# Neighbouring residual tiles summed for the feed forwards, and their first up columns taken by quarters

## The chip, the cores and the metric

The kernel runs on one core of one Trainium2 chip. The metric is the device time of one execution in microseconds (us), the median of several. All arithmetic is fp32. The engines are TensorE (PE in the profile: matmul, and PEld: the load of its weights), VectorE (DVE), ScalarE (ACT), GpSimd (POOL) and SyncE (SP, which here only issues transfers). SBUF is the on-chip memory that the engines work in, PSUM the banks that matmuls write to.

## The reference

A decoder trunk for 512 tokens of width 1024, with two layers. Layer 0 mixes with a gated DeltaNet, layer 1 with sliding-window attention; both attend to 256 memory tokens. Each layer ends with a SwiGLU feed forward:

```python
def swiglu(h, w_gate_up, w_down):
    gu = h @ w_gate_up
    return (jax.nn.silu(gu[..., :D_FF]) * gu[..., D_FF:]) @ w_down
...
        x = x + jnp.concatenate([mix_out.astype(x.dtype), mem_o.astype(x.dtype)], axis=-1) @ w_out[layer]
        x = x + swiglu(rms_norm(x, ln_ffn[layer]), w_gate_up[layer], w_down[layer])
```

D_FF is 2816, so there are 22 gate columns and 22 up columns of 128. The change touches the output projection (w_out), whose rows complete the residual x, and the feed forward behind it.

## The kernel before, in words

The residual is held transposed as eight tiles x0 to x7 of 128 features by 512 tokens. Each value that TensorE multiplies is split in a high part (whi, h, T from ScalarE) and a low part (wlo, l, a second T: the value less its high part, on VectorE), and each product is three matmuls: high by high, low of the data by high, high by low of the weights. A plain column is 8 steps over the features, so 24 matmuls of 128x512 into one bank.

Most of the feed forward goes "by quarters" (`sevens`): two columns, two halves of the features and two halves of the tokens are combined so that seven products of 128x256 do the work of eight. It needs sums of the data and of the weights. The data's sums are made by `token_sums(j)`, once per layer for four pairs of residual tiles: x_j with x_{j+4}. One call scales half of a tile (Tbh), makes four combined quarters by scalar_tensor_tensor (Tah, Tal: the two raw tiles of one pair, not parts of a split), and splits them in high parts (ScalarE) and low parts (VectorE), both named T. The weights' sums are made partly by transfers that add what they bring to a tile in SBUF (ws, issued from GpSimd's queue), partly by VectorE (wraw). The weight parts live in a ring of a few places, so that a new part can only be made when TensorE is through with an old one.

The first pair of columns is different. Its sums are not ready when the feed forward begins, so gate 0, up 0, gate 1 and up 1 are plain columns. After two steps of up 0 the squares of x, summed up (sqa) and split (ws), meet a tile of ones on TensorE, which gives the norm's rstd. Gate 0's result times rstd goes through silu (fg), the product with up is fu.

`output` computes the eight rows of w_out. In layer 1 five rows are begun before (n = 5). After each row come the residual's addition, the split of the scaled x (h, l), and the square with its addition (sq, sqa) on VectorE.

The program is recorded by a layer that sets its own order on each engine, from the dependencies and its costs; `nosync` adds a dependency of order alone. Each engine works through its own queue in order. So the order of instructions on each engine is fixed when the program is built, and only the times are found on the chip. `behind` holds weight loads on SyncE's queue back until a named instruction.

Of the kernel before, what the change touches and what calls it, by code (L numbers as in the profile page):

```python
# [9 lines left out]
F32 = mybir.dt.float32  # L10
# [8 lines left out]
P = 128  # L19
T = 512  # L20
# [64 lines left out]
class Builder:  # L85
# [980 lines left out]
    def output(self, xp, layer, mix, begun=()):  # L1066

        nc, a = self.nc, self.a
        self.weng = nc.vector
        h = []  # L1070
        self.acc = None
        hpool = self.apool if layer else self.bpool
        bank = lambda m: self.bank(("pj", "pj", "pt")[m % 3] if begun else "g" if m % 4 == 3 else "pj")
        n, ws, lows = len(begun), [], []

        def early(m):
            if begun and n <= m < KD:
                ws.append(self.weight(a["wout"][layer, m]))
                lows.append(self.low)

        done = [list(row)[-1] for row in begun]
        for i in range(2):
            early(n + i)
        for m in range(KD):
            ps = done[m] if m < n else list(
                self.row(layer, m, mix, lambda: bank(m), ws.pop(0) if ws else None))[-1]
            self.ended = self.tt(nc.vector, self.x[m], ps, self.x[m], ALU.add)
            if m >= n - 1:
                early(m + 3)
            hl = self.pair(hpool)  # L1090
            self.split_gain(self.x[m], self.gain(G_FFN[layer], m), *hl)
            if m == 0 and lows:
                self.nosync(self.low, lows[-1])
            h.append(hl)
            self.acc = self.accumulate(xp, self.acc, self.x[m], m)
        self.behind = self.loaded if layer else None
        return h

    def ffn8(self, fp, xp, layer, h, apool, rope=False):
# [121 lines left out]
            src = [a["wdn"][layer, m + i][:, f0 * P:(f0 + size) * P] for i in range(2)]  # L1221
            begin(self.sevens(fp, src, sums, ring, first, second, third, fourth, m == 0), none)

        def gate(f):
            ps = self.project(col(f, 0), h, "pj")
            if f == 0:
                list(zip(range(2), ups[0]))
                self.rstd_from(acc, *(self.t(fp, [P, T], F32R, "ws", 4) for _ in range(2)), after=self.last,
                               root=(self.cosT, self.sinT) if layer else None)
                self.use(SILU_SIN)  # L1230
            g = self.t(fp, [P, T], F32, "fg", 4)
            self.tt(nc.vector, g, ps, self.rstd, ALU.mult)
            self.fn(g, g, AF.Silu)
            return g

        f0 = 0
        for size in (8, 8, 6):
            acts, sums = [], []
            last = f0 + size == FT
            places.clear()  # L1240
            f = f0
            if f == 0:
                us, ups = [], [self.projected(col(i, 1), h, "g") for i in range(2)]
                made = act_sums()
                for i in range(2):
                    g = gate(i)
                    us.append(self.t(fp, [P, T], F32, "fu", 3))
                    if i:
                        hsums.append(self.token_sums(fp, layer, 2, h, True))
                    self.tt(nc.vector, us[i], list(ups[i])[-1], g, ALU.mult)  # L1250
                    for j in ((0, 1), (3,))[i]:
                        hsums.append(self.token_sums(fp, layer, j, h, True))
                for work in made:
                    work(*us)
                f = 2
            while f < f0 + size:
                g = columns(f, 0, (self.rstd, self.rstd), ("fg", 4), none, none, silu)
                columns(f, 1, g, ("fu", 3), *((none, none, whole) if last else act_sums(f + 2 == f0 + size)))
                f += 2
            if not last:  # L1260
                for m in range(0, KD, 2):
                    rows(m)
                    if rope and f0 + m == 0:
                        self.spread_tables()
                if f0 == 0:
                    self.t(fp, [P, 40], F32, "rest")
                f0 += size
# [57 lines left out]
    def token_sums(self, fp, layer, j, h, tags=None):  # L1325


        nc, q = self.nc, T // 2
        if j == 0:
            self.minus = self.t(fp, [P, 4], F32, "minus")  # L1330
            self.ts(self.minus, self.gains[:, G_FFN[layer] + 4:G_FFN[layer] + 8], -1.0, ALU.mult)
        g0, g1 = (self.gain(G_FFN[layer], j + i) for i in (0, 4))
        n1 = self.minus[:, j:j + 1]
        x0, x1 = self.x[j], self.x[j + 4]
        c = self.t(fp, [P, q], F32, *(("Tbh", 4) if tags else ("fc",)))
        raws = [self.t(fp, [P, T], F32, *((f"Ta{n}", 4) if tags else (f"ac{8 + j % 3}{n}",))) for n in "hl"]
        t = [raws[i // 2][:, i % 2 * q:(i % 2 + 1) * q] for i in range(4)]
        ins = nc.vector.tensor_scalar(out=c, in0=x0[:, q:], scalar1=g0, scalar2=None, op0=ALU.mult).ins
        if layer and j:

            self.nosync(ins, self.ended)
        self.stt(t[0], x0[:, :q], g0, c, ALU.mult, ALU.subtract)
        self.stt(t[1], x1[:, q:], n1, t[0], ALU.mult, ALU.subtract)
        self.stt(t[2], x1[:, q:], g1, c, ALU.mult, ALU.subtract)
        self.stt(t[3], x1[:, :q], n1, t[1], ALU.mult, ALU.subtract)
        hl = [self.t(fp, [P, D], F32R, "T", 8) for _ in range(2)]
        for i, raw in enumerate(raws):
            self.split(raw, *(x[:, i * T:(i + 1) * T] for x in hl))
        parts = {f"t{i + 1}": [x[:, i * q:(i + 1) * q] for x in hl] for i in range(4)}
        parts["11"] = [x[:, :q] for x in h[j]]  # L1350
        parts["21"], parts["22"] = ([x[:, i * q:(i + 1) * q] for x in h[j + 4]] for i in range(2))
        return parts

    def quarters(self, fp, src, sums, by, u, ring, *works):
# [24 lines left out]

        return self.sevens(fp, src, sums, ring, first, second, third, fourth)  # L1380

    def sevens(self, fp, src, sums, ring, first, second, third, fourth, late=False):

        nc = self.nc
        q, w = T // 2, len(sums) * P
        (a11, a12), (a21, a22) = ([c[:, :w], c[:, w:]] for c in src)
        a1 = self.load(src[0])
# [6 lines left out]
        nc.gpsimd.dma_start(s1, a22, accum_op=ALU.add)  # L1394
        nc.gpsimd.dma_start(s3, a21, accum_op=ALU.add)
        last = quarter("wraw", 2)
        ins = nc.sync.dma_start(last, a22).ins
        if self.behind is not None:
# [69 lines left out]
    def accumulate(self, pool, acc, x, m, out=None):  # L1468
# [218 lines left out]
def layout(i):  # L1687
# [1 line left out]
    f = lambda n: np.ascontiguousarray(i[n])  # L1689
    cols = lambda v: v.reshape(-1, P).T  # L1690

    def tiles(w, order=None):

        k, m = w.shape
        t = w.reshape(k // P, P, m // P, P).transpose(2, 1, 0, 3).reshape(m // P, P, k)
        return np.ascontiguousarray(t if order is None else t[order])

# [21 lines left out]
    for k in range(0, KD, 2):  # L1719
# [31 lines left out]
```

## Time and profile before

| | us |
|---|---|
| three executions | 1113.23, 1112.73, 1112.68 |
| median | 1112.73 |
| the profiled execution | 1112.83 |
| its span, first to last instruction | 1111.1 |

The profile shows one execution. "Busy" is the time in which an engine works on instructions; matmuls overlap, so one takes 0.39 us from start to end while the next starts 0.23 us later. A row of the timeline has the start, the time, the engine, the line of the kernel, the operation, out<-in, the shape and the count; in brackets the idle time before and what ended it. A row of groups has the count, the total and mean time, and the idle time before. A row of a window has its length and each engine's busy time with the number of instructions. Where the start of a feed forward is spoken of, layer 0's is from about 280 to 330 us and layer 1's from about 752 to 806.

### The profile page before, as it was taken

To read this page: it belongs to the slowest core of one execution; us is meant where nothing else is said; L and a number is where in the kernel's file an instruction comes from. 1 tells how busy PE (TensorE), PEld (TensorE's weight loads), DVE (VectorE), ACT (ScalarE), POOL (GpSimd) and SP (SyncE) were. 2 spreads that over 40 slices of the span, in tenths; PEclk is the share of its full clock that TensorE was granted. 3 is DMA by queue.
4 is the path that set the end of the run, shared out by engine and by line. 5 is a ranking of instruction groups with operands and counts; after the bars stand their busy time and mean duration, and the time that the engine had idled before them with its cause. 6 is when DMAs were issued, how large, how long until landed. Compare 5 with 4: busy or idle time off the path is not lost.

```text
span 1111.1 us, 21262 instructions
## 1 busy us (share of the span) xinstructions
PE 1100.6 (99%) x7957; PEld 998.9 (90%) x7957; DVE 937.0 (84%) x1890; ACT 697.2 (63%) x1470; POOL 105.9 (10%) x129
## 2 busy tenths in 40 slices
PE   9999999999999999999999999999999999999997
PEld 8888778877899999999998777788899999999996
DVE  7685977667899999999997977839999999998964
ACT  7588674466566656665565654866667466655644
POOL 0000000000011121112110000000111111121101
PEclk9999999999999999999999999999999999999999
DMA  8244352234567787778753321114677776778632
GB/s 320 98 151 142 114 142 82 90 98 145 150 173 183 189 190 191 179 184 199 191 147 99 117 74 40 58 58 142 159 176 192 189 195 184 186 198 203 148 86 90
DMA packets 81146, 165.36 MB, mean 149 GB/s; under 512 B 18588, under 2 KB 20148, under 8 KB 81044
## 3 DMA queue, kind: packets, MB, share of 16 engines
q1 hardware_dynamic: 64436, 133.87, 38.0%
q0 software_dynamic: 16320, 29.89, 16.5%
q8 instruction: 62, 1.02, 0.4%
q14 instruction: 40, 0.33, 0.1%
q10 hardware_dynamic: 288, 0.26, 0.1%
HBM read 156.98 MB, written 7.01 MB: 148 GB/s over the span
## 4 chain that ended last, share of the span: by engine, by line
PE 92%; DVE 5%; ACT 1%; issue 1%; DMA 0%; SPq 0%; DVEq 0%; ACTq 0%
PE g L144 54%; PE pj L144 26%; PE sc L144 6%; PE qk L144 3%; PE pt L144 2%; PE pt L148 1%; DVE wlo L151 1%; PE g L148 1%; DVE l L154 1%; DVE big L151 1%; DVE x L151 1%; DMA early<-in_early 0%; DVE fu L151 0%; DVE qv L154 0%; DVE btmp L151 0%
## 5 line engine op out<-in xcount | busy, mean ns | idle before, releaser
L138 ACT ACTIVATE whi<-wraw 128x512 fp32r<-128x512 f32 (+2 forms) x357 | 250.6, 711 | 161.4 <-PE g L144 66.3
L151 DVE TENSOR_TENSOR wlo<-wraw,whi 128x512 fp32r<-128x512 f32 (+2 forms) x357 | 280.5, 793 | 36.8 <-ACT whi L138 31.8
L144 PE MATMUL g<-T,whi 128*128 128x256 f32 x1280 | 228.3, 279 | 0.0
L144 PE MATMUL g<-h,wlo 128*128 128x256 f32 (+1 forms) x780 | 222.7, 285 | 0.6 <-DVE wlo L151 0.6
L144 PE MATMUL g<-l,whi 128*128 128x256 f32 (+1 forms) x780 | 222.6, 285 | 0.0
L144 PE MATMUL g<-h,whi 128*128 128x256 f32 (+1 forms) x780 | 222.4, 285 | 0.0
L144 PEld LDWEIGHTS g<-T,whi 128*128 128x128 f32 x1280 | 194.9, 188 | 0.5 <-DVE fu L154 0.5
L144 PE MATMUL pj<-h,whi 128*128 128x512 f32 (+1 forms) x460 | 182.0, 398 | 0.0
L144 PE MATMUL pj<-l,whi 128*128 128x512 f32 (+1 forms) x460 | 180.4, 393 | 0.4 <-DVE l L154 0.3
L144 PE MATMUL pj<-h,wlo 128*128 128x512 f32 (+1 forms) x460 | 179.8, 391 | 0.0
L144 PE MATMUL g<-T,wlo 128*128 128x256 f32 x640 | 178.5, 279 | 0.0
L144 PEld LDWEIGHTS g<-h,wlo 128*128 128x128 f32 x780 | 146.6, 188 | 2.8 <-DVE wlo L151 1.1
L144 PEld LDWEIGHTS g<-l,whi 128*128 128x128 f32 x780 | 146.6, 188 | 1.9
L144 PEld LDWEIGHTS g<-h,whi 128*128 128x128 f32 x780 | 146.6, 188 | 1.8
L144 PEld LDWEIGHTS g<-T,wlo 128*128 128x128 f32 x640 | 120.3, 188 | 0.0
L144 PEld LDWEIGHTS pj<-h,whi 128*128 128x128 f32 x460 | 86.4, 188 | 20.7 <-issue 4.1
L144 PEld LDWEIGHTS pj<-h,wlo 128*128 128x128 f32 x460 | 86.5, 188 | 18.0 <-issue 0.9
L144 PEld LDWEIGHTS pj<-l,whi 128*128 128x128 f32 x460 | 86.5, 188 | 17.8 <-DVE l L154 1.2
L138 ACT ACTIVATE whi<-ws 128x512 fp32r<-128x512 f32 x112 | 70.1, 626 | 38.9 <-PE g L144 36.8
L151 DVE TENSOR_TENSOR wlo<-ws,whi 128x512 fp32r<-128x512 f32 x112 | 77.1, 689 | 2.9 <-ACT whi L138 2.9
L1394 POOL DMA_DIRECT2D ws<-in_wgu x40 | 35.1, 878 | 414.6 <-DVE l L154 203.9
L138 ACT ACTIVATE fs<-g 128x256 f32<-128x256 f32 x168 | 61.5, 366 | 1.1 <-PE g L144 0.7
(398 smaller groups left out, 1929.6 us busy)
## 6 DMA issues: line engine op xcount, KB each, us to landing
wraw<-in_wgu SPq DMA_DIRECT2D x48, 512.0 KB, 4.0
ws<-in_wgu SPq DMA_DIRECT2D x80, 256.0 KB, 3.6
ws<-in_wgu POOLq DMA_DIRECT2D x80, 256.0 KB, 4.9
wraw<-in_win SPq DMA_DIRECT2D x26, 512.0 KB, 4.0
wraw<-in_wgu SPq DMA_DIRECT2D x40, 256.0 KB, 5.4
wraw<-in_wout SPq DMA_DIRECT2D x16, 512.0 KB, 3.4
ws<-in_wdn SPq DMA_DIRECT2D x32, 256.0 KB, 5.7
wraw<-in_wdn SPq DMA_DIRECT2D x16, 512.0 KB, 3.8
```

Of the source, the lines that this page charges most:

```text
L138: self.copied = self.nc.scalar.activation(out, in_, AF.Copy, **kw).ins
L144: return self.nc.tensor.matmul(out, lhsT, rhs, start=start, stop=stop, skip_group_check=more).ins
L148: return self.nc.tensor.transpose(out, in_, self.ident[:k, :k]).ins
L151: return eng.tensor_tensor(out=out, in0=a, in1=b, op=op).ins
L154: return self.nc.vector.scalar_tensor_tensor(out=out, in0=in0, scalar=scalar, in1=in1, op0=op0, op1=op1).ins
L1394: nc.gpsimd.dma_start(s1, a22, accum_op=ALU.add)
```

## The change

1. `token_sums(j)` takes the neighbours x_2j and x_2j+1 instead of x_j and x_{j+4}. The rows of the feed forward's gate and up weights are laid out in the order 0, 2, 4, 6, 1, 3, 5, 7 for that; the plain gate columns still go through the features from 0 to 7. Pairs 0 to 2 are made while rows 6 and 7 of the output are computed, pair 3 after x7.
2. Up columns 0 and 1 are taken by quarters. A new `gates` computes gate 0, two steps of gate 1, rstd, pair 3 of the sums, the rest of gate 1, and then come the seven products. Their two transfers from SyncE (ws) and two that accumulate (GpSimd) are issued before.
3. The low parts of the sums of pairs 0 to 2 go from VectorE to GpSimd, the scaling Tbh from VectorE to ScalarE. In layer 1 the additions of squares for x1 to x4 go to GpSimd.
4. In layer 0's output the first two steps of row 7, six matmuls, are taken before row 5.

```diff
@@ output
+            if not begun and m == KD - 3:
+                tail = self.row(layer, KD - 1, mix, lambda: bank(KD - 1))
+                list(zip(range(2), tail))
...
-            self.acc = self.accumulate(xp, self.acc, self.x[m], m)
+            self.acc = self.accumulate(xp, self.acc, self.x[m], m, eng=nc.gpsimd if 0 < m < n else None)
@@ ffn8
-        def gate(f):
...
+        def gates(w):
+            halves = h[::2] + h[1::2]
+            order = [i % 2 * 4 + i // 2 for i in range(KD)]
+            steps = [self.projected(col(f, 0), halves, "pj", order, None if f else w) for f in range(2)]
+            done = [list(steps[0])[-1]]
+            list(zip(range(2), steps[1]))
+            self.rstd_from(acc, *(self.t(fp, [P, T], F32R, "ws", 4) for _ in range(2)), after=self.last,
+                           root=(self.cosT, self.sinT) if layer else None)
+            self.use(SILU_SIN)
+            hsums.append(self.token_sums(fp, layer, 3, h, True))
+            done.append(list(steps[1])[-1])
...
-                us, ups = [], [self.projected(col(i, 1), h, "g") for i in range(2)]
...
+                steps = self.quarters(fp, [col(i, 1) for i in range(2)], hsums, by, us, ring, *works[:-1], ahead=True)
+                next(steps)
+                self.behind = self.behind if layer else None
+                for j in range(3):
+                    hsums.append(self.token_sums(fp, layer, j, h, True))
+                by.extend(gates(w))
+                begin(steps, lambda: works[-1](*us))
@@ token_sums
-        x0, x1 = self.x[j], self.x[j + 4]
+        x0, x1 = self.x[2 * j:2 * j + 2]
...
-        ins = nc.vector.tensor_scalar(out=c, in0=x0[:, q:], scalar1=g0, scalar2=None, op0=ALU.mult).ins
+        self.copy(c, x0[:, q:], scale=g0)
...
-            self.split(raw, *(x[:, i * T:(i + 1) * T] for x in hl))
+            self.split(raw, *(x[:, i * T:(i + 1) * T] for x in hl), nc.gpsimd if j < 3 else None)
@@ sevens
-        nc.gpsimd.dma_start(s1, a22, accum_op=ALU.add)
-        nc.gpsimd.dma_start(s3, a21, accum_op=ALU.add)
+        for to, part in ((s1, a22), (s3, a21)):
+            ins = nc.gpsimd.dma_start(to, part, accum_op=ALU.add).ins
+            if ahead and self.pooled is not None:
+                self.nosync(ins, self.pooled)
+        if ahead:
+            yield
+            a1 = self.load(src[0])
@@ accumulate
-        self.tt(self.nc.vector, nxt, acc, sq, ALU.add)
+        ins = self.tt(eng or self.nc.vector, nxt, acc, sq, ALU.add)
@@ layout
-        "wgu": np.stack([tiles(w, pair) for w in gu]),
+        "wgu": np.stack([tiles(w, pair, [0, 2, 4, 6, 1, 3, 5, 7]) for w in gu]),
```

How this stands on the engines, at three places. The first is GpSimd's queue where layer 0's feed forward begins. Before, the accumulating transfers of the first gate pair and the next follow the two tables of layer 1's rotary positions:

```order
L1509 MEMSET sinT_2785 128x512
L1510 MEMSET cosT_2784 128x512
L1394 DMA ws_3341<-in_wgu 128x512
L1395 DMA ws_3342<-in_wgu 128x512
L1394 DMA ws_3460<-in_wgu 128x512
L1395 DMA ws_3461<-in_wgu 128x512
```

Now:

```order
L1524 MEMSET sinT_2785 128x512
L1525 MEMSET cosT_2784 128x512
L1403 DMA ws_3121<-in_wgu 128x512
L1403 DMA ws_3122<-in_wgu 128x512
L151 ISA
L151 TENSOR_TENSOR T_3138<-Tah_3130,T_3137 128x512
L151 TENSOR_TENSOR T_3138<-Tal_3131,T_3137 128x512
L151 TENSOR_TENSOR T_3152<-Tah_3144,T_3151 128x512
L151 TENSOR_TENSOR T_3152<-Tal_3145,T_3151 128x512
L151 TENSOR_TENSOR T_3166<-Tah_3158,T_3165 128x512
L151 TENSOR_TENSOR T_3166<-Tal_3159,T_3165 128x512
L1403 DMA ws_3386<-in_wgu 128x512
```

The up pair's two transfers come first, then the six low parts, and the gate pair's transfers (from ws_3386 on) stand behind them. In layer 1 four additions of squares stand ahead of the same sequence.

The second place is VectorE around x7 of layer 0 (x_531_2774 is x7, l_3097 its low part, which gate 0 needs; ws is the low part of the summed squares). Before:

```order
L154 SCALAR_TENSOR_TENSOR Tal_3194<-x_528_2771,minus_3190,Tah_3193 128x256
L151 TENSOR_TENSOR x_531_2774<-g_3070,x_531_2774 128x512
L151 TENSOR_TENSOR T_3201<-Tah_3193,T_3200 128x512
L154 SCALAR_TENSOR_TENSOR Tah_3207<-x_529_2772,minus_3190,Tah_3207 128x256
L154 SCALAR_TENSOR_TENSOR l_3097<-x_531_2774,gains_67,h_3096 128x512
L151 TENSOR_TENSOR sqa_3102<-sqa_3062,sq_3100 128x512
L151 TENSOR_TENSOR T_3201<-Tal_3194,T_3200 128x512
L154 SCALAR_TENSOR_TENSOR Tal_3208<-x_529_2772,gains_67,Tbh_3206 128x256
L151 TENSOR_TENSOR ws_3158<-sqa_3102,ws_3157 128x512
```

Now:

```order
L154 SCALAR_TENSOR_TENSOR Tal_3159<-x_529_2772,minus_3127,Tah_3158 128x256
L151 TENSOR_TENSOR x_531_2774<-g_2990,x_531_2774 128x512
L151 TENSOR_TENSOR wlo_3199<-wraw_3196,whi_3198 128x1024
L154 SCALAR_TENSOR_TENSOR l_3097<-x_531_2774,gains_67,h_3096 128x512
L151 TENSOR_TENSOR sqa_3102<-sqa_3075,sq_3100 128x512
L154 SCALAR_TENSOR_TENSOR Tah_3220<-x_530_2773,gains_67,Tbh_3219 128x256
L154 SCALAR_TENSOR_TENSOR Tal_3221<-x_531_2774,gains_67,Tbh_3219 128x256
L151 TENSOR_TENSOR ws_3210<-sqa_3102,ws_3209 128x512
```

Between x7's addition and l stands the low part of gate 1's weights instead of a low part and a step of the sums; behind l there are two steps of pair 3 ahead of ws instead of a low part and one step. All steps of pairs 0 to 2 are ahead of x7 now.

The third place is TensorE behind the gates of layer 0 (h_3096 and l_3097 are x7's parts, h_2818 x0's). Before, up 0 ends and gate 1 begins:

```order
L144 MATMUL g_3150<-h_3096,whi_3146 128x512
L144 MATMUL g_3150<-l_3097,whi_3146 128x512
L144 MATMUL g_3150<-h_3096,wlo_3147 128x512
L144 MATMUL pj_3226<-h_2818,whi_3222 128x512
L144 MATMUL pj_3226<-l_2819,whi_3222 128x512
L144 MATMUL pj_3226<-h_2818,wlo_3223 128x512
```

Now at the same count of matmuls gate 1 ends and the up pair's first product begins:

```order
L144 MATMUL pj_3202<-h_3096,whi_3198 128x512
L144 MATMUL pj_3202<-l_3097,whi_3198 128x512
L144 MATMUL pj_3202<-h_3096,wlo_3199 128x512
L144 MATMUL g_3261<-h_2818,whi_3264 128x256
L144 MATMUL g_3261<-l_2819,whi_3264 128x256
L144 MATMUL g_3261<-h_2818,wlo_3265 128x256
```

Gate 1 has moved into up 0's place, and 84 matmuls of 128x256 follow in the place of two plain columns.

More of the change, by code (lines that the diff above doesn't have):

```diff
@@ L1070, in output @@
         h = []
-        self.acc = None
+        self.acc = self.pooled = None
         hpool = self.apool if layer else self.bpool
@@ L1083, in output @@
             early(n + i)
+        tail = None
         for m in range(KD):
-            ps = done[m] if m < n else list(
+            if not begun and m == KD - 3:
+                tail = self.row(layer, KD - 1, mix, lambda: bank(KD - 1))
+                list(zip(range(2), tail))
+            ps = done[m] if m < n else list(tail if tail is not None and m == KD - 1 else
                 self.row(layer, m, mix, lambda: bank(m), ws.pop(0) if ws else None))[-1]
@@ L1222, in rows @@
             begin(self.sevens(fp, src, sums, ring, first, second, third, fourth, m == 0), none)
-        def gate(f):
[L1225 to L1234, printed above, removed]
+        def gates(w):
[9 more added lines that the diff above has]
+            done.append(list(steps[1])[-1])
+            for ps in done:
+                g = self.t(fp, [P, T], F32, "fg", 4)
+                self.tt(nc.vector, g, ps, self.rstd, ALU.mult)
+                self.fn(g, g, AF.Silu)
+                yield g
         f0 = 0
@@ L1242, in ffn8 @@
             if f == 0:
-                us, ups = [], [self.projected(col(i, 1), h, "g") for i in range(2)]
[L1244 to L1254, printed above, removed]
+                w = self.weight(col(0, 0))
+                self.behind = self.loaded
+                by, works = [], act_sums()
+                us = [self.t(fp, [P, T], F32, "fu", 3) for _ in range(2)]
+                steps = self.quarters(fp, [col(i, 1) for i in range(2)], hsums, by, us, ring, *works[:-1], ahead=True)
[5 more added lines that the diff above has]
+                begin(steps, lambda: works[-1](*us))
                 f = 2
@@ L1330, in token_sums @@
             self.minus = self.t(fp, [P, 4], F32, "minus")
-            self.ts(self.minus, self.gains[:, G_FFN[layer] + 4:G_FFN[layer] + 8], -1.0, ALU.mult)
-        g0, g1 = (self.gain(G_FFN[layer], j + i) for i in (0, 4))
+            self.ts(self.minus, self.gains[:, G_FFN[layer] + 1:G_FFN[layer] + KD:2], -1.0, ALU.mult)
+        g0, g1 = (self.gain(G_FFN[layer], 2 * j + i) for i in range(2))
         n1 = self.minus[:, j:j + 1]
-        x0, x1 = self.x[j], self.x[j + 4]
+        x0, x1 = self.x[2 * j:2 * j + 2]
         c = self.t(fp, [P, q], F32, *(("Tbh", 4) if tags else ("fc",)))
@@ L1337, in token_sums @@
         t = [raws[i // 2][:, i % 2 * q:(i % 2 + 1) * q] for i in range(4)]
-        ins = nc.vector.tensor_scalar(out=c, in0=x0[:, q:], scalar1=g0, scalar2=None, op0=ALU.mult).ins
-        if layer and j:
-            self.nosync(ins, self.ended)
+        self.copy(c, x0[:, q:], scale=g0)
+        if layer and j == 3:
+            self.nosync(self.copied, self.ended)
         self.stt(t[0], x0[:, :q], g0, c, ALU.mult, ALU.subtract)
@@ L1347, in token_sums, with quarters @@
         for i, raw in enumerate(raws):
-            self.split(raw, *(x[:, i * T:(i + 1) * T] for x in hl))
+            self.split(raw, *(x[:, i * T:(i + 1) * T] for x in hl), nc.gpsimd if j < 3 else None)
         parts = {f"t{i + 1}": [x[:, i * q:(i + 1) * q] for x in hl] for i in range(4)}
-        parts["11"] = [x[:, :q] for x in h[j]]
-        parts["21"], parts["22"] = ([x[:, i * q:(i + 1) * q] for x in h[j + 4]] for i in range(2))
+        parts["11"] = [x[:, :q] for x in h[2 * j]]
+        parts["21"], parts["22"] = ([x[:, i * q:(i + 1) * q] for x in h[2 * j + 1]] for i in range(2))
         return parts
-    def quarters(self, fp, src, sums, by, u, ring, *works):
+    def quarters(self, fp, src, sums, by, u, ring, *works, **kw):
         nc = self.nc
@@ L1378, in fourth, with sevens @@
             self.stt(u[1][:, :q], pa, -1.0, by[1][:, :q], ALU.mult, ALU.mult)
-        return self.sevens(fp, src, sums, ring, first, second, third, fourth)
-    def sevens(self, fp, src, sums, ring, first, second, third, fourth, late=False):
+        return self.sevens(fp, src, sums, ring, first, second, third, fourth, **kw)
+    def sevens(self, fp, src, sums, ring, first, second, third, fourth, late=False, ahead=False):
         nc = self.nc
-        q, w = T // 2, len(sums) * P
+        q, w = T // 2, src[0].shape[1] // 2
         (a11, a12), (a21, a22) = ([c[:, :w], c[:, w:]] for c in src)
-        a1 = self.load(src[0])
+        a1 = None if ahead else self.load(src[0])
         quarter = lambda *kind: self.t(fp, [P, T], F32, *kind)[:, :w]
@@ L1466, in rstd_from, with accumulate @@
         self.nc.scalar.activation(self.floor, self.root, AF.Square, scale=math.sqrt(EPS * D / P))
-    def accumulate(self, pool, acc, x, m, out=None):
+    def accumulate(self, pool, acc, x, m, out=None, eng=None):
         n = x.shape[1]
@@ L1475, in accumulate @@
         nxt = self.t(pool, [P, T], F32, "sqa", 2) if out is None else out
-        self.tt(self.nc.vector, nxt, acc, sq, ALU.add)
+        ins = self.tt(eng or self.nc.vector, nxt, acc, sq, ALU.add)
+        if eng is not None:
+            self.pooled = ins
         return nxt
@@ L1690, in layout, with tiles @@
     cols = lambda v: v.reshape(-1, P).T
-    def tiles(w, order=None):
+    def tiles(w, order=None, rows=None):
         k, m = w.shape
+        if rows is not None:
+            w = w.reshape(k // P, P, m)[rows].reshape(k, m)
         t = w.reshape(k // P, P, m // P, P).transpose(2, 1, 0, 3).reshape(m // P, P, k)
```

## The prediction

> **What bounds the kernel now.** I read the page's totals first, then the chain of work that ended last, then single stretches and the list of waits. The page says how busy each engine was and on which engine the chain ran.
>
> ```profile
> span 1111.1 us, 21262 instructions
> ...
> PE 1100.6 (99%) x7957; PEld 998.9 (90%) x7957; DVE 937.0 (84%) x1890; ACT 697.2 (63%) x1470; POOL 105.9 (10%) x129
> ...
> PE 92%; DVE 5%; ACT 1%; issue 1%; DMA 0%; SPq 0%; DVEq 0%; ACTq 0%
> ```
>
> TensorE is busy for 99% of the span and holds 92% of the chain. So a matmul saved is time saved, if nothing new makes TensorE wait. The change sits in two places, the start of each feed forward. These rows give the busy time in the two starts and in the steady part of layer 1, and the list of TensorE's waits from 280 to 400.
>
> ```profile
> 295.00:330.00 35.00, 35.00 (x203) 30.88 (x202) 34.05 (x67) 22.94 (x41) 5.34 (x6) 1.00 0.64 167
> 760.00:800.00 40.00, 40.00 (x204) 34.13 (x203) 39.89 (x74) 28.53 (x49) 4.45 (x5) 1.00 0.59 157
> 806.00:846.00 40.00, 40.00 (x345) 40.00 (x344) 38.68 (x79) 26.22 (x56) 7.02 (x8) 1.00 0.74 186
> ...
> PE g L144 <- DVE wlo L151: 0.4, 1, 0.4
> ```
>
> After the length come TensorE, its weight loads, VectorE (DVE), ScalarE (ACT), GpSimd (POOL), then the granted clock, 1.00 throughout. TensorE never stops at either start. VectorE hardly does either: 34.05 of 35 us, then 39.89 of 40. It is the engine that decides whether a saving of TensorE can be kept. ScalarE has 12 of 35 us free, GpSimd nearly 30.
>
> **TensorE's part.** A matmul's cost is the spacing of starts, not its duration. The rows are two 512-wide matmuls 74 starts apart and two 256-wide ones 28 groups of three, so 84 starts, apart.
>
> ```profile
> 284.12 0.39 PE L144 MATMUL pj<-h,whi 128*128 128x512 f32 x1
> ...
> 300.89 0.39 PE L144 MATMUL pj<-h,wlo 128*128 128x512 f32 x1
> ...
> 350.02 0.28 PE L144 MATMUL g<-T,wlo 128*128 128x256 f32 x1
> ...
> 359.82 0.28 PE L144 MATMUL g<-T,wlo 128*128 128x256 f32 x1
> ```
>
> That is 16.77/74 = 0.2266 us and 9.80/84 = 0.1167 us. Two plain up columns are 2 x 8 x 3 = 48 matmuls of 512, 10.88 us. By quarters they are 7 products x 4 x 3 = 84 of 256, 9.80 us. Each layer saves 1.08 us, both 2.16. No other matmul is added or removed; the six matmuls of row 7 that go ahead of row 5 are only moved.
>
> **VectorE's part.** The next rows give its durations around the last residual tile x7 of layer 0, and the two idle times that follow.
>
> ```profile
> 297.02 0.69 DVE L151 TENSOR_TENSOR x<-g,x 128x512 f32<-128x512 f32 x1
> ...
> 298.61 0.75 DVE L154 SCALAR_TENSOR_TENSOR l<-x,gains,h 128x512 fp32r<-128x512 f32 x1
> 299.28 0.69 DVE L151 TENSOR_TENSOR sqa<-sqa,sq 128x512 f32<-128x512 f32 x1
> 299.88 0.69 DVE L151 TENSOR_TENSOR T<-Tal,T 128x512 fp32r<-128x512 f32 x1
> 300.48 0.48 DVE L154 SCALAR_TENSOR_TENSOR Tal<-x,gains,Tbh 128x256 f32<-128x256 f32 x1
> ...
> 302.48 1.22 DVE L151 TENSOR_TENSOR wlo<-wraw,whi 128x1024 fp32r<-128x1024 f32 x1
> 303.61 0.69 DVE L151 TENSOR_TENSOR T<-Tal,T 128x512 fp32r<-128x512 f32 x1
> 304.21 0.35 DVE L1338 TENSOR_SCALAR Tbh<-x,gains 128x256 f32<-128x256 f32 x1
> 304.48 1.22 DVE L151 TENSOR_TENSOR wlo<-wraw,whi 128x1024 fp32r<-128x1024 f32 x1
> ...
> 318.83 0.69 DVE L151 TENSOR_TENSOR fu<-g,fg 128x512 f32<-128x512 f32 x1 [0.70 <-PE g L144]
> ...
> 321.38 0.42 DVE L154 SCALAR_TENSOR_TENSOR tmp<-fu,tmp 128x256 f32<-128x256 f32 x1
> 321.71 0.69 DVE L151 TENSOR_TENSOR wlo<-ws,whi 128x512 fp32r<-128x512 f32 x1
> ...
> 334.31 0.69 DVE L151 TENSOR_TENSOR wlo<-wraw,whi 128x512 fp32r<-128x512 f32 x1 [0.90 <-ACT whi L138]
> ```
>
> From start to start, 512 wide costs 0.60, 1024 wide 1.13, the 256-wide steps of the sums 0.40, other 256-wide ones 0.33, the scaling Tbh 0.27. Per layer these leave VectorE: 6 low parts of the sums (3.60), 4 Tbh (1.08), 2 products of 512 (1.20), 2 weight low parts of 1024 (2.26), together 8.14. These come: 7 weight low parts of 512 (4.20), 2 weight sums (1.20), 5 steps of 256 (1.65), 1 of 512 (0.60), together 7.65. So 0.5 us less in layer 0. In layer 1 four additions of squares go too, 2.40, which makes 2.9.
>
> VectorE thus gains 0.5 in layer 0 where TensorE gains 1.08; the 0.6 that is missing comes out of its lead. It has 0.70 idle at 318.83 and 0.90 at 334.31, so 1.6 in reserve, and I charge nothing. If the reserve couldn't be used, 0.6 of the gain is lost.
>
> What could stop TensorE, point by point in the new order, layer 0, with the durations above: (a) The low part l of x7. Before, it is ready at 298.61 + 0.75 = 299.36; the second matmul of gate 0's eighth step takes it, 22 starts after 296.36, so at 301.35. Now one weight low part (1.13) stands ahead of it instead of a low part of sums and a step (1.00): ready about 299.5, lead 1.8. (b) The sum of squares ws feeds the two matmuls with ones, after 30 starts, at 303.16; behind l come an addition and two steps, so it is ready about 301.5, lead 1.6. (c) The up pair begins when both gates are through, 48 + 2 starts after 296.36, at 307.7; its first weights are ready about 302.7, and later ones 3 to 5 us ahead. (d) The first gate pair follows at 316.1 = 307.7 + 8.4 (72 of the 84; the last quarter is taken in the next pair's course); the smallest lead I find on VectorE there is 1.9. So nothing waits if VectorE and GpSimd keep these durations.
>
> Layer 1 starts with these rows: x7's low part, and the matmul that takes it.
>
> ```profile
> 773.51 0.75 DVE L154 SCALAR_TENSOR_TENSOR l<-x,gains,h 128x512 fp32r<-128x512 f32 x1
> ...
> 776.50 0.39 PE L144 MATMUL pj<-l,whi 128*128 128x512 f32 x1
> ```
>
> The lead is 2.2 now. The new order puts more steps of the sums ahead of it, and ScalarE's h of x6 stands behind a weight part that waits for a transfer; my chain brings l to about 775.2, lead 1.3. Behind it the leads are 4 and more, since VectorE has 2.9 less to do.
>
> **ScalarE's part.** It takes 4 Tbh, 3 copies fs and 7 weight parts of 512 for 2 of 1024. Rows, 290 to 330:
>
> ```profile
> L138 ACT ACTIVATE whi<-wraw 128x512 fp32r<-128x512 f32 x9 | 5.6, 630 | 4.7 <-PE g L144 3.6 <-DMA wraw<-in_wgu 0.5 <-DVE wraw L151 0.3
> L138 ACT ACTIVATE whi<-wraw 128x1024 fp32r<-128x1024 f32 x3 | 3.2, 1051 | 3.2 <-PE pj L144 3.2
> L138 ACT ACTIVATE fs<-g 128x256 f32<-128x256 f32 x4 | 1.5, 363 | 0.0
> L138 ACT ACTIVATE Tbh<-tmp 128x256 fp32r<-128x256 f32 x1 | 0.4, 403 | 0.0
> ```
>
> 4 x 0.40 + 3 x 0.36 + 7 x 0.63 - 2 x 1.05 = 5.0 us. The 12 idle us cover it; if they didn't, weights would come late by at most these 5.
>
> **GpSimd's part.** It gets 6 low parts of 128x512 in layer 0, and 6 with 4 additions of squares in layer 1. Before, it does such work only at the end, on 128x256. The rows show it there, VectorE at the same time, and its transfers at the start of layer 0.
>
> ```profile
> 300.93 0.92 POOL L1394 DMA_DIRECT2D ws<-in_wgu  x1 [36.76 <-DMA ws<-in_wgu]
> ...
> 1100.18 1.44 POOL L151 TENSOR_TENSOR T<-T,ws 128x256 f32<-128x256 f32 x2 [54.35 <-ACT ws L132]
> ...
> 1099.84 1.35 DVE L151 TENSOR_TENSOR T<-T,g 128x256 f32<-128x256 f32 x3 [1.64 <-ACT g L132]
> ...
> 1101.44 0.74 DVE L151 TENSOR_TENSOR T<-T,g 128x256 f32<-128x256 f32 x2
> ...
> ws<-in_wgu POOLq DMA_DIRECT2D x80, 256.0 KB, 4.9
> ```
>
> One of 256 takes half of 1.44, so 0.72; one of 512 between 0.72 and 1.44. I take 1.4, as if length counted in full. Layer 0: the first raw sums are ready about 292.4, the last about 298; six take 8.6, so the last low part is there by about 305. The up pair's second product takes it at about 309.9. In layer 1 I get 778.2 against 785. The transfers that accumulate weights for the gate pair stand behind these in GpSimd's queue: issued at 306 with 0.9, landing 4.9 later, at about 312, and needed as weights at 317.5. Two more of them per layer, for the up pair, go ahead of the low parts, while GpSimd idles (36.76 us before 300.93). SyncE's four extra loads in both layers are weights asked for one stage earlier; the engines' memory share is 0.64 and 0.59 there, and I charge nothing; one late by its whole landing time would cost up to 4.9.
>
> The sum: 1112.83 (the profiled execution: its span 1111.1 and 1.73 around it) - 2.16 + 0 = 1110.67. That execution is 0.10 above the median of 1112.73, so 1110.6 there. A difference of 0.2%, 2.2 us, is about what a measurement of this kernel can tell from no change; 2.16 lies on that line.
>
> **The unknown price: GpSimd beside VectorE.** At 1100.18 VectorE's operations keep 0.42 us while GpSimd computes, but they read one input from a matmul's bank (g). At the two starts VectorE's steps read both inputs from SBUF, and no row shows that beside GpSimd. Below: no loss, as in these rows; a gain is excluded, since no wait goes. Above: VectorE stops for all of every GpSimd operation, 6 x 1.4 = 8.4 and 10 x 1.4 = 14 us. I take nothing, from the only rows that show both engines at work.
>
> The Trainium skill has a rule that speaks against this, "SBUF — State Buffer", section "Who interferes with whom": a VectorE instruction with both inputs in SBUF contends with a GpSimd instruction that reads SBUF, and whichever issues first holds the shared ports for its whole length while the other stops. The rows at 1100 agree with its other half, that an instruction with at most one SBUF input doesn't contend; the half that counts here no row shows. By it the sum would be the first rival's.
>
> **Rivals.** First, slower: VectorE stops while GpSimd reads. In layer 0 8.4 us against the smallest lead of 1.9 leaves 6.5 on TensorE, in layer 1 14 against 4 leaves 10; less 2.16 that is 1112.7 + 14.3 = 1127 at full price. At half, 4.2 - 1.9 and 7 - 4 leave 5.3: 1116. It turns the sign when each of the 16 operations stops VectorE for over some 0.5 us: 6 x 0.5 - 1.9 + 10 x 0.5 - 4 = 2.1. For it speaks that VectorE is 97% to 99.7% busy just there; against it the rows at 1100, as far as they reach.
>
> Second, VectorE is the bound in layer 0 and its reserve can't be used: 0.6 lost, 1111.2 or, if the wait of 0.4 above grows by as much again, 1111.6. For it speaks that wait; against it the 0.70 and 0.90 of idle time.
>
> Third, slower by lateness alone: the accumulating transfers, behind six operations, land after 317.5. They have 5 us; it needs operations of over 2.2 us, three times the length of the 256-wide ones. Or ScalarE's queue holds up h of x7 in layer 1, lead 1.3. About 1113 to 1116.
>
> Fourth, more than forecast: the relief of VectorE in layer 1 (2.9) removes the 0.4 kind of waits in the feed forwards, 1109.8.
>
> **How the numbers follow.** Forecast, 1110.0 to 1111.0: 0.56, and as it lies on the line of 0.2%, 0.30 of it faster and 0.26 same. More: 0.08, faster. VectorE's 0.6: 0.10, same. Stops beside GpSimd: 0.20, slower, half of it above 1117. Late transfers or ScalarE: 0.06, slower. Faster 0.38, same 0.36, slower 0.26. The range leaves out the upper half of the stops and the lowest part of the fourth: 1109.8 to 1117. The forecast's own range is 1110.0 to 1111.0.
>
> **What the changed profile would show.** Right: from 307 on 84 matmuls of 256 in place of the second up column, TensorE 35.00 of 35 busy in 295:330, no new row in the list of TensorE's waits at either start, GpSimd's low parts at about 1.4, VectorE's steps of the sums still at 0.48 and weight low parts at 0.69 beside them. Wrong: steps of 1 us and more beside GpSimd's operations; TensorE waiting for l of x7, for wlo near 303 to 318 or 775 to 800, or for ScalarE's h; GpSimd's transfers landing after 317.

## The result, and the profile after

The changed kernel takes 1130.46 us in the median (1128.41 to 1131.78) against 1112.70 for the kernel before on the same chip: a ratio of 1.0158, 95% interval 1.0146 to 1.0170. It is slower by 17.8 us where 2.2 less was forecast. The profiled execution took 1130.69. Its page:

```profile
span 1128.9 us, 21490 instructions
...
PE 1104.1 (98%) x8029; PEld 1004.0 (89%) x8029; DVE 950.0 (84%) x1888; ACT 706.9 (63%) x1494; POOL 132.3 (12%) x149
...
PE 63%; DVE 6%; issue 1%; ACT 1%; DMA 1%; DVEq 0%; ACTq 0%
```

TensorE's share of the chain has fallen from 92% to 63%, and VectorE does two instructions less in 13 us more. TensorE's list of waits, first from 280 to 400, then from 750 to 880, where before there was one entry of 0.4:

```profile
PE g L144 <- ACT fs L138: 4.0, 1, 4.0
PE pj L144 <- ACT h L138: 0.8, 1, 0.8
PE pj L144 <- DVE l L154: 0.5, 1, 0.5
...
PE pj L144 <- ACT h L138: 6.6, 1, 6.6
PE pj L144 <- DVE l L154: 2.9, 1, 2.9
```

The list names ScalarE first. The timeline of VectorE in layer 0 shows what made it late, with GpSimd's beside it:

```profile
292.83 0.68 DVE L151 TENSOR_TENSOR x<-pj,x 128x512 f32<-128x512 f32 x1
293.43 0.92 DVE L154 SCALAR_TENSOR_TENSOR Tal<-x,gains,Tbh 128x256 f32<-128x256 f32 x1
294.27 1.51 DVE L154 SCALAR_TENSOR_TENSOR Tal<-x,minus,Tah 128x256 f32<-128x256 f32 x1
295.70 1.52 DVE L154 SCALAR_TENSOR_TENSOR Tah<-x,gains,Tbh 128x256 f32<-128x256 f32 x1
297.14 1.78 DVE L154 SCALAR_TENSOR_TENSOR l<-x,gains,h 128x512 fp32r<-128x512 f32 x1
298.85 0.68 DVE L151 TENSOR_TENSOR sqa<-sqa,sq 128x512 f32<-128x512 f32 x1
...
292.47 1.59 POOL L151 TENSOR_TENSOR T<-Tah,T 128x512 fp32r<-128x512 f32 x1 [0.94 <-PE pj L144]
294.03 1.48 POOL L151 TENSOR_TENSOR T<-Tal,T 128x512 fp32r<-128x512 f32 x1
295.63 1.31 POOL L151 TENSOR_TENSOR T<-Tah,T 128x512 fp32r<-128x512 f32 x1
296.90 1.48 POOL L151 TENSOR_TENSOR T<-Tal,T 128x512 fp32r<-128x512 f32 x1
```

A step of the sums that takes 0.48 alone takes 1.51, and l 1.78 instead of 0.75. Each ends 0.3 to 0.5 us after one of GpSimd's: the rows read as if the two engines took turns, one instruction each. Two rows are the key. The residual's addition at 292.83 reads one input from a matmul's bank, has GpSimd beside it, and keeps its 0.68. At 298.85 GpSimd has nothing to do, and VectorE is at its usual time again.

In layer 0 six instructions are longer, by 0.44, 1.03, 1.04, 1.03, 1.05 and 1.09 us, together 5.7; in layer 1 ten, by 9.0. That is 14.7 us for 16 GpSimd operations, 0.92 each. Each had relieved VectorE of 0.60, 9.6 in all. So the move left VectorE 5 us busier.

How this reached TensorE in layer 1, on ScalarE:

```profile
772.41 0.89 ACT L138 ACTIVATE Tbh<-x,gains 128x256 f32<-128x256 f32 x2
779.88 1.06 ACT L138 ACTIVATE whi<-wraw 128x1024 fp32r<-128x1024 f32 x1 [6.58 <-DMA wraw<-in_wgu]
780.85 0.70 ACT L138 ACTIVATE h<-x,gains 128x512 fp32r<-128x512 f32 x1
...
781.59 0.75 DVE L154 SCALAR_TENSOR_TENSOR l<-x,gains,h 128x512 fp32r<-128x512 f32 x1 [3.03 <-ACT h L138]
...
788.28 0.68 DVE L151 TENSOR_TENSOR x<-pj,x 128x512 f32<-128x512 f32 x1
```

The weight part waits for a load, and h of x6, ready to be made since 777.4, stands behind it. The load (on SyncE's queue at 773.34) needed a place that a low part of weights on VectorE freed; that one took 2.32 us instead of 1.22, from 770.99 to 773.31, beside the last addition of squares. With it, four stops of 3.5 us together stand on VectorE ahead of the load, and h of x6 is made 3.5 us late.

TensorE's wait of 6.6 us is not for this h but for h of x7, one tile later. VectorE waits 3.03 us for h of x6; then GpSimd stops three steps of the sums for 1.0 us each, and so VectorE adds x7 only at 788.28. The wait of 2.9 for l of x7 follows in the same way: two instructions ahead of l are stopped, and l itself.

Last, the granted clock (the number behind the five busy times) in two stretches after long waits:

```profile
317.00:320.00 3.00, 3.00 (x17) 3.00 (x16) 1.51 (x4) 1.21 (x4) 0.45 (x1) 0.50 0.98 300
794.00:798.00 4.00, 4.00 (x10) 3.13 (x10) 4.00 (x9) 2.30 (x4) 0.00 (x0) 0.50 0.14 58
```

TensorE runs at half its clock there: for 3.4 us in layer 0, and in layer 1 from about 788 to 798, for about half of which it waits anyway. Counted from start to start of the matmuls, the long waits cost 6.0 us in layer 0 and 10.2 in layer 1, and the half clock 1.8 and 2.0: 20.0 us. Less the 2.16 of saved matmuls that is 17.8, the difference of the spans (1128.9 - 1111.1).

### The profile page after: what moved, and what is told of

It is laid out like the page before. It is cut to its first block, busy times and chain, and to the rows that moved or that the text cites. A ratio compares the mean times of both kernels' runs of the same rounds, so it can differ in the third digit from the quotient of the medians.

```text
span 1128.9 us, 21490 instructions
## 1 busy us (share of the span) xinstructions
PE 1104.1 (98%) x8029; PEld 1004.0 (89%) x8029; DVE 950.0 (84%) x1888; ACT 706.9 (63%) x1494; POOL 132.3 (12%) x149
## 3 DMA queue, kind: packets, MB, share of 16 engines
q8 instruction: 63, 1.03, 0.4%
## 4 chain that ended last, share of the span: by engine, by line
PE 63%; DVE 6%; issue 1%; ACT 1%; DMA 1%; DVEq 0%; ACTq 0%
PE g L144 48%; PE pj L144 10%; PE qk L144 3%; DVE wlo L151 2%; PE pt L144 1%; PE pt L148 1%; DVE l L154 1%; DVE x L151 1%; DVE fu L151 1%; DMA wraw<-in_wgu 1%; ACT h L138 0%; DVE Tal L154 0%; DVE Tah L154 0%; DVE sqa L151 0%; DVE wraw L151 0%
## 5 line engine op out<-in xcount | busy, mean ns | idle before, releaser
L138 ACT ACTIVATE whi<-wraw 128x512 fp32r<-128x512 f32 (+2 forms) x363 | 253.5, 705 | 164.0 <-PE g L144 71.3
L151 DVE TENSOR_TENSOR wlo<-wraw,whi 128x512 fp32r<-128x512 f32 (+2 forms) x363 | 284.7, 791 | 37.2 <-ACT whi L138 32.1
L144 PE MATMUL g<-T,whi 128*128 128x256 f32 x1344 | 240.8, 280 | 4.0 <-ACT fs L138 4.0
L144 PE MATMUL g<-h,wlo 128*128 128x256 f32 (+1 forms) x772 | 217.2, 281 | 0.6 <-DVE wlo L151 0.6
L144 PE MATMUL g<-h,whi 128*128 128x256 f32 (+1 forms) x772 | 217.0, 281 | 0.0
L144 PE MATMUL g<-l,whi 128*128 128x256 f32 (+1 forms) x772 | 217.0, 281 | 0.0
L144 PEld LDWEIGHTS g<-T,whi 128*128 128x128 f32 x1344 | 205.3, 189 | 4.7 <-ACT fs L138 4.2
L144 PE MATMUL g<-T,wlo 128*128 128x256 f32 x672 | 188.0, 280 | 0.0
L144 PEld LDWEIGHTS g<-T,wlo 128*128 128x128 f32 x672 | 126.8, 189 | 0.0
L1403 POOL DMA_DIRECT2D ws<-in_wgu x84 | 73.2, 884 | 334.5 <-DVE wlo L151 114.8
```

Of the source, the lines that this page charges most:

```text
L138: self.copied = self.nc.scalar.activation(out, in_, AF.Copy, **kw).ins
L144: return self.nc.tensor.matmul(out, lhsT, rhs, start=start, stop=stop, skip_group_check=more).ins
L151: return eng.tensor_tensor(out=out, in0=a, in1=b, op=op).ins
L1403: ins = nc.gpsimd.dma_start(to, part, accum_op=ALU.add).ins
```

## The experiments

Theory A: a GpSimd instruction that reads SBUF stops VectorE's instructions that need the same way in, for about its own length, and what stands behind them comes late. Rival B: the new order alone does it, above all ScalarE's h behind a weight part. Most of these runs vary by 2 to 5 us from one execution to the next, so differences of 1 us between them decide nothing.

**e1, no arithmetic on GpSimd at the starts.**

```diff
-            self.split(raw, *(x[:, i * T:(i + 1) * T] for x in hl), nc.gpsimd if j < 3 else None)
+            self.split(raw, *(x[:, i * T:(i + 1) * T] for x in hl), None)
-            self.acc = self.accumulate(xp, self.acc, self.x[m], m, eng=nc.gpsimd if 0 < m < n else None)
+            self.acc = self.accumulate(xp, self.acc, self.x[m], m, eng=None)
```

> The changed kernel, but the low parts of the sums and layer 1's squares are back on VectorE, so GpSimd has no arithmetic at the two starts. Theory A (a GpSimd instruction that reads SBUF stops VectorE's two-input instructions for its own length, and what is behind them gets late): no VectorE instruction at the starts is longer than its usual time, the waits of 6.8 and 3.4 us in layer 1 and of 4.2 in layer 0 go; VectorE has about 3.1 us more than in the kernel before in each layer against leads of 2 to 3, so some 0 to 1.5 us of new waits per layer: 1110.6 to 1114. Rival B (the new order itself, ScalarE's h behind a weight part whose load is issued late): layer 1's wait of 6.8 us stays, 1120 or more.

Measured 1117.51 us (1116.16 to 1119.24), ratio 1.0042 (1.0027 to 1.0057): 13 us of the 17.8 are gone. The waits for h and for fs are gone, against B. But it ends above A's range and is still slower than the kernel before. TensorE's waits in layer 1, and the busy times from 752 to 792:

```profile
PE pj L144 <- DVE wlo L151: 2.6, 1, 2.6
...
752.00:792.00 40.00, 37.32 (x187) 31.31 (x186) 38.95 (x66) 31.29 (x52) 3.58 (x4) 1.00 0.51 139
...
752.00:792.00 40.00, 40.00 (x178) 33.07 (x177) 39.26 (x67) 28.43 (x43) 3.58 (x4) 1.00 0.57 158
```

The last row is the kernel before: VectorE is as full there, 39.26 of 40 us, and TensorE doesn't wait. So the share alone tells little. In e1 the timeline lists no idle time of VectorE from 757 to 787, and TensorE waits for it. Without GpSimd's help the change gives VectorE 3.1 us more per layer by the prediction's count, and in layer 1 the low part of gate 1's weights comes late; in layer 0 the waits are only 0.4 in all. One thing is not separated: the recording layer has also laid VectorE's queue anew in e1.

**e2 and e3, one half of it each.** e2 takes back only the second pair of lines of e1's diff, the squares; e3 only the first, the low parts.

> The changed kernel with only layer 1's four additions of squares back on VectorE; the low parts stay on GpSimd. Theory A: four stops of about 1 us and the late load behind them go from layer 1, the wait for ScalarE's h (6.8 us) falls to 3 or less, layer 0 stays as it is (6 us of waits): 1122 to 1127. Rival B: the wait for h stays near 6.8 and VectorE's 2.4 us come on top: 1130 to 1132.

> The changed kernel with only the low parts back on VectorE; the squares stay on GpSimd. Theory A: layer 0 has no stops, its waits go to 0 to 1.5 us; in layer 1 the four stops ahead of x6 remain and with them most of the wait for h: 1117 to 1123. Rival B: layer 1 as in the changed kernel, 1122 to 1124, and so also for A's upper end; what tells them apart is VectorE's instruction times ahead of x6 (A: about 1 us longer beside each square) and run e2.

e2 took 1126.63 us (ratio 1.0124, 1.0107 to 1.0140), e3 1121.65 (1.0082, 1.0067 to 1.0097); both as A said. In e2 layer 0 keeps its waits of 4.0, 0.8 and 0.5; in layer 1 the wait for h is gone, but one of 2.8 for gate 1's low part comes instead. In e3 layer 0 has no wait above 0.8; ahead of x6 in layer 1 four instructions of VectorE are 0.5 to 1.1 us longer, as A said, and a wait for h of 2.9 is left. So the squares' four stops make the wait for h (of x7 here too), and the low parts more than double it.

**e4 and e5, reads and writes of GpSimd in the kernel before.** To the kernel before, work is added that nothing uses. e4 reads; e5 fills.

```diff
+            if j < 3:
+                for s in (slice(0, 224), slice(224, 448)):
+                    self.tt(nc.gpsimd, self.t(fp, [P, 224], F32, "spare", 1), raw[:, s],
+                            hl[0][:, i * T:(i + 1) * T].bitcast(F32)[:, s], ALU.subtract)
```

```diff
+            if j < 3:
+                for n in range(5):
+                    ins = nc.gpsimd.memset(self.t(fp, [P, 224], F32, "spare", 1), 0.0).ins
...                 # the first of five waits for the high part of the sums
```

> The kernel before, with work added that nothing uses: for pairs 0 to 2 GpSimd computes each low part of the sums a second time (two pieces of 128x224) into a spare tile, VectorE still does its own. VectorE's and ScalarE's instructions and order stay, but for one swap. Theory A: 24 pieces of about 0.65 us, VectorE's two-input steps beside them get 0.4 to 0.6 us longer each, some 5 us per layer against a lead of about 2 to 3: waits of 1 to 4 us per layer, 1115 to 1121. If GpSimd's reads don't stop VectorE: 1112.7, at most a microsecond more from the transfers behind them.

> The control to e4: the kernel before, with GpSimd filling a spare tile of 128x224 thirty times per layer, five fills behind each high part of pairs 0 to 2, so at the same places and for about the same time, but with instructions that only write. Theory A (reads stop VectorE): VectorE's instructions keep 0.48 and 0.69 us, no new wait of TensorE: 1112 to 1114. If any GpSimd instruction beside VectorE stops it: as e4, 1120 or more.

e4 took 1128.44 us, e5 1118.13: with the same tiles in the same places, 10.3 us between reading and writing. The same three instructions of VectorE and GpSimd's beside them, e4 first:

```profile
299.76 1.16 DVE L151 TENSOR_TENSOR T<-Tal,T 128x512 fp32r<-128x512 f32 x1
300.83 0.89 DVE L154 SCALAR_TENSOR_TENSOR Tal<-x,gains,Tbh 128x256 f32<-128x256 f32 x1
301.64 1.16 DVE L151 TENSOR_TENSOR ws<-sqa,ws 128x512 fp32r<-128x512 f32 x1
...
299.17 2.26 POOL L151 TENSOR_TENSOR spare<-Tal,T 128x224 f32<-128x224 f32 x2 [0.89 <-ACT T L138]
```

```profile
299.31 0.69 DVE L151 TENSOR_TENSOR T<-Tal,T 128x512 fp32r<-128x512 f32 x1
299.91 0.48 DVE L154 SCALAR_TENSOR_TENSOR Tal<-x,gains,Tbh 128x256 f32<-128x256 f32 x1
300.31 0.69 DVE L151 TENSOR_TENSOR ws<-sqa,ws 128x512 fp32r<-128x512 f32 x1
...
299.13 4.41 POOL L1351 MEMSET spare<- 128x224 f32 x13 [1.00 <-ACT T L138]
```

GpSimd is busy beside VectorE in both. Beside reads VectorE's instructions are 0.41 to 0.47 longer, beside fills not at all. In e5 TensorE has no wait at either start; in e4 it waits 2.6 in layer 0, and 2.3 and 1.4 in layer 1. That settles A's first half, the stops: they need no change of order beyond one swap. e4 itself came out above A's range of 1115 to 1121; 5 us of that are the tile's (e10, below). Against e5 its waits of 6.3 and two spells of half clock make up most of the 10.3. GpSimd pays too: the two pieces of 224 shown take 1.1 us each, while e4's shortest took 0.67.

e5's total was not as expected, since its matmuls start every 118.4 ns instead of 116.7.

**e10, the spare tile alone**, with one fill per layer.

> The kernel before with the spare tile of e4 and e5 (896 bytes of each partition, which moves the tiles behind it) and one fill per layer in place of thirty. In e5 no wait of TensorE is left, but its 256-wide matmuls start every 118.4 ns instead of 116.7 through both feed forwards. If the tiles' new places do that: 118.4 again and 1117 to 1118.5. If the fills did it: 116.7 and 1112.7.

1118.09 us, ratio 1.0043 (1.0026 to 1.0059), and 118.3 ns from start to start: the 5 us come with the tile and not with the fills. That they come because its 896 bytes of each partition move the tiles behind it is inferred. Windows of 10 us, e10 and then the kernel before (one of the 87 or 88 matmuls may lie on the edge):

```profile
900.00:910.00 10.00, 10.00 (x87) 10.00 (x86) 8.88 (x17) 6.05 (x13) 1.95 (x3) 1.00 0.81 206
...
900.00:910.00 10.00, 10.00 (x88) 10.00 (x87) 9.09 (x17) 6.79 (x13) 2.53 (x3) 1.00 0.86 230
```

So e4 must be read against e5, not against the kernel before.

**e6, e7 and e8, on e1: what bounds it then.** e6 makes gate 1's weights ahead of the sums, e7 leaves out part 4, e8 puts Tbh back on VectorE.

```diff
-                w = self.weight(col(0, 0))
+                w = [self.weight(col(f, 0)) for f in range(2)]
...
-            if not begun and m == KD - 3:
+            if False and m == KD - 3:
...
-        self.copy(c, x0[:, q:], scale=g0)
+        ins = nc.vector.tensor_scalar(out=c, in0=x0[:, q:], scalar1=g0, scalar2=None, op0=ALU.mult).ins
```

> e1 (all arithmetic on VectorE) with the weights of gate 1 made directly behind those of gate 0, ahead of the sums. In e1 their low part stands behind two pairs of sums on VectorE and TensorE waits 2.7 us for it in layer 1. If VectorE's load bounds the start (theory): that wait goes, but VectorE's work is the same, so about half comes back at the up pair or later: 1114 to 1117. If it was the place alone (rival): all 2.7 to 3.5 us come back, 1112.5 to 1114.

> e1 without part 4: row 7 of layer 0's output is taken whole, behind row 6. Only layer 0 changes. If the six matmuls ahead of row 5 give VectorE room between x6 and x7: x6 and its low part come 1.4 us later to the sums and layer 0 loses up to 1 us: 1117.5 to 1118.5. If they do nothing: as e1, 1117.5.

> e1 with the scaling Tbh back on VectorE (part 3's other half): 4 x 0.27 = 1.1 us more on VectorE per layer, 1.6 less on ScalarE. If VectorE's load bounds the starts: 0.5 to 2 us longer than e1, 1118 to 1119.5. If not: as e1, 1117.5.

e6 took 1117.47 us (1116.07 to 1118.49), no less than e1, just above its expected range. The wait for gate 1's weights is gone, and its layer 1 has these instead:

```profile
PE g L144 <- DVE ws L151: 1.5, 1, 1.5
PE g L144 <- DVE wlo L151: 0.7, 1, 0.7
```

All waits at the two starts come to 3.7 us in e1 and 3.4 in e6. A wait moved along VectorE's queue comes up at the next place, which speaks for the load as the bound and against the place. e8 took 1120.52 (1118.12 to 1122.15), longer than e1 by 3 where 0.5 to 2 were expected; e1's wait of 2.6 is 3.2 there, and a spell of half clock follows. But the intervals of the two ratios overlap (e8: 1.0049 to 1.0084), and the profile of e8 also has a long stretch of slower matmuls (last section), so e8 shows little about the load. e7 took 1121.55 (1119.49 to 1123.76), 4 more than e1 where at most 1 was expected: without the six matmuls ahead of row 5 the summed squares come late, and TensorE waits 2.5 for ws in layer 0, again with a spell of half clock behind. Layer 1 has e1's wait of 2.6 unchanged, but here a spell of half clock follows it too, which part 4 doesn't touch. Part 4 is worth something, and I had taken it for nothing.

**e9, the changed kernel with h of x6 ahead of the weight part.**

```diff
+            if m == KD - 2:
+                self.sixth = self.copied
...
+            w1 = self.weight(col(1, 0))
+            if layer:
+                self.nosync(self.copied, self.sixth)
```

> The changed kernel (GpSimd as changed) with one order of ScalarE altered in layer 1: the high part of gate 1's weights, whose load lands late, stands behind h of x6 instead of ahead of it. Theory A says that the 6.8 us wait for h is the stops by GpSimd made longer on their way: VectorE's low part is late, so the load that needs its place, so the weight part, and h behind it. Then h comes when x6 is there, the wait for h falls to 1 to 2 us, VectorE gets x6's low part some 4 us earlier, and the time falls by 3 to 6 us: 1124 to 1127.5. If h was late for another reason: 1130.

1131.22 us (1127.78 to 1132.37), no gain against the changed kernel, against my expectation. VectorE's wait of 3.03 for h of x6 went, but GpSimd's operations now meet other instructions ahead of x7. Layer 1's waits:

```profile
PE pj L144 <- ACT h L138: 4.3, 1, 4.3
PE pj L144 <- DVE l L154: 3.0, 1, 3.0
```

The 4.3 are for h of x7, whose residual VectorE added at 785.80. So in this execution the order on ScalarE accounts for 2.3 of the 6.6; I put the rest down to VectorE's lost time. The profiled execution is 2.9 shorter than the changed kernel's, the other three are not; how much the order is worth is not settled.

No version of the change beat the kernel before. e1 and e6 came nearest, and their layer 1 suggests why: the quarters of one more pair need 3.1 us of VectorE where it has no idle time. The waits there, 3.3 and 2.4, are more than the 2.16 saved.

## Why the prediction was wrong

TensorE's part was right in itself: 84 matmuls of 256, 116.7 ns apart as before, stand in the place of 48 of 512, and the account above closes with 2.16 saved.

The step that failed is "the unknown price": "I take nothing, from the only rows that show both engines at work". Those rows had VectorE with one input in a bank. The truth lay nearer the end that I put at the top, 1.4 us per operation: 0.92 was measured, 14.7 us in all for a term that I had put at nothing. The row nearest in engines was the wrong one to price by; the one that decides is what each instruction reads. The Trainium skill's rule ("SBUF — State Buffer", "Who interferes with whom") said so, and the runs agree: in the changed kernel two inputs in SBUF beside a GpSimd read took 0.41 to 1.10 us longer, one input in a bank 0.00, and in e5 a GpSimd fill cost 0.00. For one input the rule there excepts VectorE's two-port modes; the prediction left that condition out, and the last section has instructions with one tensor as input that were stopped.

The first rival was therefore the case that came, at a chance of 0.20. That its price of 1127 at full stops lies close to 1130.46 is partly luck: 0.92 came instead of 1.4 by 16 operations, it set a lead of 4 against layer 1's stops where the prediction's own lead for l of x7 was 1.3, and it lacked two things.

The first is ScalarE's order, which passes the stops on. "The 12 idle us cover it" counted time and not order. In layer 0 rstd, the function table and silu stand ahead of the copy fs in ScalarE's queue:

```profile
308.70 0.64 ACT L138 ACTIVATE T<-Tal 128x512 fp32r<-128x512 f32 x1 [1.47 <-DVE Tal L154]
...
309.75 0.67 ACT L132 ACTIVATE rstd<-g,eps 128x512 f32<-128x512 f32 x1
...
312.28 1.28 ACT L123 ACT_TABLE_LOAD   x1
...
316.25 0.36 ACT L138 ACTIVATE fs<-g 128x256 f32<-128x256 f32 x1
```

T waits for a step that GpSimd had stopped, rstd comes after it at 309.75, although the matmuls with ones began at 305.12 and end within 0.7 us, and fs 6.5 us later: rstd is 4.0 late, as long as TensorE's wait. In e1 fs follows rstd by the same 6.5 us (303.81, 310.27) and nothing waits for it. So ScalarE's added work cost nothing by itself; it took the stops to make it late.

The second is the clock: after a long wait TensorE runs at 0.50 for a while, 3.8 us in all, which no term had.

How good VectorE's ledger was stays open in part. In e1 VectorE has 3.6 us of low parts more than the ledger in layer 0, and 2.4 of squares besides in layer 1. Layer 0 waits for only 0.4 us, so its reserve was larger than the leads of 1.6 to 1.9 said; layer 1 waits for 3.3. The second rival, VectorE as the bound, spoke of layer 0; e1 shows such a bound in layer 1, and with more work on VectorE than the changed kernel gives it. The third named late transfers or h of x7 in layer 1, and that is where the longest wait came, but as a step of the first rival's chain: the load took 6.5 us from 773.34 to ScalarE's start at 779.88, where this kind of load has a median of 4.0 in the profile before and 5.3 in the one after. The fourth, more than forecast, had nothing for it. GpSimd's own length was right: its low parts took 1.41 and 1.57 us in the mean of the two kinds (from Tah and from Tal), turns included, for the 1.4 taken.

## What to carry to other kernels

Before work is moved to GpSimd beside a busy VectorE, look at what both read: where GpSimd reads SBUF and VectorE has both inputs there, each operation of 128x512 moved here took 0.6 us from VectorE and gave back 0.9. Where the trace shows two engines side by side without harm, ask whether the operands lie where those of the new place will lie. And an engine's idle time covers added work only if the order of its queue lets it: the urgent instruction waits behind whatever stands ahead of it.

## What I had not expected of the hardware

A scaling with a single tensor as input is stopped too: Tbh took 0.75 us in e4 beside GpSimd's reads and 0.35 in e5, and the negated gains of 128x4 took 0.66 in the changed kernel's layer 1 against 0.17 before.

The half clock comes after waits of quite different length: after 4.0 us in the changed kernel's layer 0, after 2.3 in e4's layer 1, but not after the 2.6 of e1. e7 has that very wait, 2.56 us for the same low part, and behind it the clock is 0.50 from 783.0 to 786.4. So the length of the wait alone doesn't decide it. The Trainium skill ("TensorE: Matmul & The Clock Gate", Part 1) has the clock halved after an idle window of some 3.4 us and freed after a busy one. The spells of 3.4 us agree (the changed kernel's of some 10 us in layer 1 has waits within it); waits of 2.3 are shorter than that window.

The spacing of 256-wide matmuls isn't one number. It is 116.7 ns in the profiles before and after, 118.3 where 896 bytes were put ahead of the tiles (e4, e5, e10), and in e1 117.8 between about 390 and 510 only, though no tile was added. The profiles of e2, e3, e6 and e8 have such stretches too, e8's from about 810 to 1070. The first comes with the added tile. For the second I have no cause; it is worth over 1 us in e1 and over 2 in e8, and no run isolated it. Such stretches and the spells of half clock blur comparisons of a few us between e1, e6, e7 and e8.
